# A two-layer trunk on one core: modulation steps moved from the input stage into the attention, and the second layer's weight loads and splits put in another order

## The chip, the cores and the metric

The kernel runs on one core of one Trainium2 chip, as one program of some 28,000 instructions. The metric is device time in microseconds (us), lower is better. The core's engines are PE (TensorE, the matrix products), DVE (VectorE), ACT (ScalarE), POOL (GpSimd) and SP, whose queue issues most of the DMA transfers. Each engine goes through its own list of instructions in order, and waits for the others by semaphores; a transfer queue is gone through in order too.

## The reference

One inference step of two layers over 512 sample tokens and 128 prompt tokens, model width 1024. Layer 0 has latent attention (MLA) with 12 heads, layer 1 a neighbourhood attention with 8 heads beside a windowed attention with 8. Cut to what matters:

```python
def reference(...):
    for l in range(DEPTH):                               # DEPTH = 2
        mp = adaln(c_ctx[None, :], w_mod[l], b_mod[l])   # 6 columns of 1024: mp[:, 0] .. mp[:, 5]
        ms = adaln(c, w_mod[l], b_mod[l])                # (silu(c) @ w_mod + b_mod)
        hp = modulate(rmsnorm(xp, norm_mix[l]), mp[:, 0], mp[:, 1])
        hs = modulate(rmsnorm(xs, norm_mix[l]), ms[:, 0], ms[:, 1])
        op, os_ = ...                                    # in-projection, attention, @ w_out
        xp = xp + mp[:, 2] * op
        xs = xs + ms[:, 2] * os_
        hp = modulate(rmsnorm(xp, norm_ffn[l]), mp[:, 3], mp[:, 4])
        hs = modulate(rmsnorm(xs, norm_ffn[l]), ms[:, 3], ms[:, 4])
        xp = xp + mp[:, 5] * conv_ffn(hp, w_up[l], conv_w[l], conv_b[l], w_down[l])
        xs = xs + ms[:, 5] * conv_ffn(hs, w_up[l], conv_w[l], conv_b[l], w_down[l])
    return rmsnorm(xp, norm_final), rmsnorm(xs, norm_final), ...   # and the new caches
```

## The kernel before

**Layout.** Activations are kept transposed: 128 of the 1024 features in the partitions, 642 columns for the 512 + 128 tokens and two spare ones. They are worked in two halves, 352 and 290 columns in layer 0 (names ending in `a` and `b`, `ha` and `hb`) and 322 and 320 in layer 1. A product of full precision takes a weight and an activation as a high part and a low part: ACT casts the high part (line 117, `whi` from `raw`), and DVE or POOL subtracts it to get the low part (line 113, `wlo`); PE then makes three products (high with high, low with high, high with low).

**The modulation columns.** `w_mod` has 2 layers of 6 columns of 1024, m = 0 to 5. A column cannot be had by an ordinary product without loading PE for one token, so it is summed in *steps*: a step is one load of 128 rows of one column (`mraw`, 512 or 256 wide), and for each of the two conditioning vectors a multiply and an add into `acc`. The first vector's add is one instruction on DVE (line 316). The second vector's is the same on DVE in the form `m.d`, and otherwise a multiply on ACT (line 313) and an add on POOL (line 314). The first step of eight is a multiply only (line 310, ACT). The eighth is followed by a transposition (line 325) and a reduction (line 326) on DVE for each vector, into `mred`. When a column's parts are all reduced, `mod_finish` has PE move them into place (line 337). The list `todo` gives the order of steps. Column m = 2 of layer 0 is needed first in the output product, m = 3 and 4 in the norm after it.

**Layer 0's input stage** (`mla_in`) follows a table of names, `MLA_IN`, written out by hand: one list for all engines, each name issuing a piece of work. `m` and `m.d` issue a modulation step, with loads on ACT's queue; `p` a block of products; `nw.q.0` and `nw.q.1` the norm's factors for the two halves of the query latents; `sc` and `lo` their high and low parts (`qan`); `xc`, `xa`, `xb`, `xm` work on the pooling branch. After the table, `mla` makes the first four query products, whose evacuation on DVE is line 774 (`q` from `tr` and a table) and line 113.

**Layer 0's attention** (`mla`) goes through 26 units (12 heads by two halves, and two more rounds in which the last units drain). Each unit follows one of the two tables `MLA_UNITS`, even or odd. It has one score block (`sc`, maxima at line 808), the exponentials, the turned probabilities (`pt`, line 843) and the weighted sums (`o`, lines 866 and 868). In an even unit `m` stands three times, in an odd one once; from unit 2 on each `m` issues a modulation step, at most `MLA_MODS` = 32 in all, so the units from 18 on issue none. Here the steps are 256 wide and their loads are on SP's queue.

**Layer 0's output product** (`out_proj`) is not written out by hand: a scheduler with its own costs sets the order on the engines. For each of eight `j` it loads `x`, and the weight `wo`, in two rings.

**Layer 1's attention** ends in the table `ODD_END`. `fo` loads an early weight of the output product, `fs` splits it, `pa` splits a group of finished outputs (`o32`) into `ha`, `hb` high and low, in both halves, by `put_act`. After the table the splits that remain are made. **Layer 1's closing stage** is in the class `Mix`: `begin` makes the output product, j = 0 and 1 with the early weights, and j from 2 on with weights loaded by `load` and split by `parts`. Its order of loads is that of the code: x (`load_x`, with a fill of two columns by POOL) and raw weights in turn on SP's queue. The last part of the kernel goes through slots of the up-projection (`slot`), in which `block("S2")` is a block of low parts and `u3` a piece of the convolution on DVE.

## Time and profile before

| what | us |
|---|---|
| runs, median (lowest to highest) | 1706.52 (1704.79 to 1714.16), three runs |
| profiled execution, its own time | 1716.46 |
| its span, first to last instruction | 1714.7, granted clock 0.971 |
| input stage of layer 0, its last part with steps | 93.5 to 142 |
| attention of layer 0, units 2 to 17, with steps | to 308.6 |
| attention of layer 0, units 18 to 25, without | 308.6 to 358 |
| output product of layer 0 | from 358 on |
| layer 1's attention ends, closing stage starts | about 1160 to 1189 |

The profiled execution is about 10 us slower than the median of the runs. A row of a timeline gives the start, the length, the engine, the line, what is written from what, and in brackets how long the engine was idle before it and what ended that idle time. A row of a table by stage gives the stretch, its length, the busy time and the instructions of each engine, the granted clock of PE, the share of the DMA engines and GB/s.

### The profile page before, as it was taken

Reading aid. Unit: us, or ns where it says so; the run is one execution under the profiler, and the core shown is the slowest. Engines: PE = TensorE matmul, PEld = TensorE weight load, DVE = VectorE, ACT = ScalarE, POOL = GpSimd, SP = SyncE. Lnnn points to the kernel's source line nnn. Section 1 sums busy time; section 2 is a strip of 40 time slices with the busy share of each in tenths; the row PEclk is TensorE's granted clock in tenths of the full one; section 3 lists DMA queues with packets and bytes.
Section 4 is the critical chain, followed back from the end, with each engine's and each line's share of the span. In section 5 each row is a group of like instructions: output and inputs, shape, how many; then the busy total and the mean of one; then the engine's idle time right before and its main releaser. Section 6 shows DMA issues by size and latency. Waiting matters only on the chain.

```text
span 1714.7 us, 28130 instructions
## 1 busy us (share of the span) xinstructions
PE 1588.6 (93%) x10349; PEld 1514.9 (88%) x10349; DVE 1266.2 (74%) x2183; ACT 929.1 (54%) x1792; POOL 776.2 (45%) x711
## 2 busy tenths in 40 slices
PE   8877888888999999999998999987997999999996
PEld 2777777788999999999997999986997999999996
DVE  4886788768899778977638777774687667777766
ACT  3554767645655335533445677874465344444435
POOL 2154677554234333433063244655235455555443
PEclk9998999989999999999999999998999999999999
DMA  9431212053344444544235211114222223222221
GB/s 339 136 105 49 62 51 80 13 174 124 117 148 145 153 139 143 155 152 136 68 107 169 59 50 53 50 39 138 86 84 75 78 73 98 82 77 73 78 73 63
DMA packets 79032, 175.62 MB, mean 102 GB/s; under 512 B 11598, under 2 KB 29342, under 8 KB 78894
## 3 DMA queue, kind: packets, MB, share of 16 engines
q1 hardware_dynamic: 76398, 169.55, 30.8%
q10 hardware_dynamic: 2304, 4.20, 0.7%
q8 instruction: 82, 1.34, 0.3%
q14 instruction: 56, 0.46, 0.1%
q0 software_dynamic: 192, 0.07, 0.0%
HBM read 166.71 MB, written 8.03 MB: 102 GB/s over the span
## 4 chain that ended last, share of the span: by engine, by line
PE 54%; DVE 12%; issue 6%; ACT 4%; POOL 3%; DMA 3%; SPq 0%; DVEq 0%; POOLq 0%; ACTq 0%
PE mm L137 26%; PE p L1594 22%; DMA mraw<-in_w_mod_dram 2%; DVE acc L316 1%; PE sc L1209 1%; DVE wlo L113 1%; PE tr L1247 1%; PE o L1259 1%; DVE nt L424 1%; DMA raw<-in_w_out_dram 1%; POOL w L113 1%; DVE ha L438 1%; ACT whi L117 1%; PE sc L137 0%; PE o L851 0%
## 5 line engine op out<-in xcount | busy, mean ns | idle before, releaser
L314 POOL TENSOR_TENSOR acc<-acc,mt 128x512 f32<-128x512 f32 x115 | 175.9, 1530 | 266.3 <-ACT mt L313 251.5
L137 PE MATMUL mm<-ha,whi 128*128 128x352 f32 (+1 forms) x1168 | 288.7, 329 | 4.7 <-ACT ha L437 4.6
L137 PE MATMUL mm<-hb,whi 128*128 128x290 f32 (+1 forms) x1168 | 244.9, 303 | 1.1 <-ACT hb L437 1.1
L137 PEld LDWEIGHTS mm<-ha,whi 128*128 128x128 f32 (+1 forms) x1168 | 203.3, 191 | 6.6 <-ACT ha L437 4.7
L316 DVE SCALAR_TENSOR_TENSOR acc<-mraw,cs,acc 128x512 f32<-128x512 f32 (+1 forms) x165 | 170.5, 1040 | 48.0 <-DMA mraw<-in_w_mod_dram 46.4
L137 PEld LDWEIGHTS mm<-hb,whi 128*128 128x128 f32 (+1 forms) x1168 | 193.6, 192 | 3.9 <-issue 2.7
L137 PE MATMUL mm<-ha,wlo 128*128 128x352 f32 (+1 forms) x584 | 189.5, 325 | 0.0
L113 POOL TENSOR_TENSOR wlo<-raw,whi 128x1024 fp32r<-128x1024 f32 (+3 forms) x47 | 100.5, 2143 | 175.1 <-ACT whi L117 107.2
L137 PE MATMUL mm<-hb,wlo 128*128 128x290 f32 (+1 forms) x584 | 175.2, 300 | 0.0
L113 POOL TENSOR_TENSOR w<-raw,w 128x512 fp32r<-128x512 f32 (+1 forms) x68 | 89.5, 1327 | 177.0 <-ACT w L117 177.0
L137 PE MATMUL mm<-g,whi 128*128 128x352 f32 (+1 forms) x704 | 157.5, 311 | 6.5 <-DVE x L447 5.2
L117 ACT CAST whi<-raw 128x1024 fp32r<-128x1024 f32 (+3 forms) x117 | 115.9, 995 | 69.0 <-PE mm L137 52.7
L313 ACT ACTIVATE mt<-mraw,cs 128x512 f32<-128x512 f32 x115 | 81.8, 721 | 111.7 <-DMA mraw<-in_w_mod_dram 99.4
L1594 PE MATMUL p<-g,d 128*128 128x320 f32 (+1 forms) x912 | 140.4, 312 | 1.0 <-POOL d L113 0.9
L1594 PEld LDWEIGHTS p<-g,d 128*128 128x128 f32 x912 | 136.9, 190 | 2.5 <-POOL d L113 2.1
L1594 PE MATMUL p<-hb,w 128*128 128x322 f32 (+1 forms) x816 | 129.5, 313 | 7.8 <-DVE cg L1965 6.5
L1594 PEld LDWEIGHTS p<-hb,w 128*128 128x128 f32 x816 | 123.5, 191 | 9.0 <-DVE cg L1965 6.8
L1594 PE MATMUL p<-ha,w 128*128 128x322 f32 x768 | 123.0, 315 | 5.8 <-ACT w L117 4.0
L137 PEld LDWEIGHTS mm<-g,whi 128*128 128x128 f32 x704 | 118.3, 189 | 8.6 <-ACT ha L437 3.8
L1594 PEld LDWEIGHTS p<-ha,w 128*128 128x128 f32 x768 | 117.5, 192 | 6.8 <-ACT w L117 4.3
L137 PEld LDWEIGHTS mm<-hb,wlo 128*128 128x128 f32 (+1 forms) x584 | 112.8, 193 | 0.0
L137 PEld LDWEIGHTS mm<-ha,wlo 128*128 128x128 f32 (+1 forms) x584 | 110.4, 189 | 0.5
(332 smaller groups left out, 3773.7 us busy)
## 6 DMA issues: line engine op xcount, KB each, us to landing
raw<-in_w_up_dram SPq DMA_DIRECT2D x90, 512.0 KB, 3.6
mraw<-in_w_mod_dram SPq DMA_DIRECT2D x128, 256.0 KB, 2.9
raw<-in_w_out_dram SPq DMA_DIRECT2D x19, 512.0 KB, 4.2
raw<-in_w_in_odd_dram SPq DMA_DIRECT2D x18, 512.0 KB, 3.5
mraw<-in_w_mod_dram SPq DMA_DIRECT2D x16, 512.0 KB, 8.8
raw<-in_w_down_dram SPq DMA_DIRECT2D x16, 512.0 KB, 3.6
draw<-in_w_down_dram SPq DMA_DIRECT2D x40, 192.0 KB, 2.4
raw<-in_w_down_dram SPq DMA_DIRECT2D x16, 384.0 KB, 3.1
```

Of the source, the lines that this page charges most:

```text
L113: (engine or self.nc.vector).tensor_sub(lo, src, Fv(hi))
L117: self.nc.scalar.copy(hi, src)
L137: self.pe = self.nc.tensor.matmul(out, lhsT=l, rhs=r, start=k == 0, stop=k == n - 1)
L313: nc.scalar.activation(t, raw, AF.Copy, scale=s)
L314: nc.gpsimd.tensor_add(acc, acc, t)
L316: nc.vector.scalar_tensor_tensor(out=acc, in0=raw, scalar=s, in1=acc, op0=ALU.mult, op1=ALU.add)
L424: self.nc.vector.scalar_tensor_tensor(out=t[:, c], in0=x[k][:, c0:c1][:, c], scalar=self.mod[l][:, ma, k, v : v + 1], in1=rs[:, c], op0=AL ...
L438: nc.vector.scalar_tensor_tensor(out=lo[:, c], in0=t[:, c], scalar=ss, in1=Fv(hi[:, c]), op0=ALU.add, op1=ALU.subtract)
L1209: nc.tensor.matmul(ps[:, c : c + n], lhsT=u.Q[:, a], rhs=x[e], start=e == 0, stop=e == 1)
L1247: nc.tensor.transpose(tp[:, j * P : (j + 1) * P], u.p[b][:, x : x + P], self.ident)
L1259: nc.tensor.matmul(u.o[:, u.t[c][2]], lhsT=v, rhs=u.t[c][e], start=c == 0 and e == 0, stop=c == 4 and e == 1)
L1594: self.t.pe = self.nc.tensor.matmul(ps[:, 0:n], lhsT=l_, rhs=r[:, 0:n], start=first and m == 0, stop=last and m == count - 1, skip_group_c ...
```

## The change

- Input stage: the table `MLA_IN` loses eight of its 16 modulation steps (the second half of column 2), on DVE 11 accumulations, two transposes and two reductions. `xc.1` stands earlier and `nw.q.1` behind it, after the first half's low parts.
- Attention of layer 0: `MLA_MODS` goes from 32 to 48. The eight removed steps of 512 columns become 16 of 256, since `todo` gives the second half of column 2 in pieces of 256. They come first there, and all others later in turn, until unit 25. `mod_finish` at unit 2 and after the attention go.
- Output product of layer 0: two x loads at first and each next x ahead, and the raw of a weight loaded one `j` ahead.
- End of layer 1's attention: the second early weight's low part is made on DVE instead of POOL; `pa` splits the first half alone, and the second halves follow after the table, on ACT and DVE.
- Closing stage of layer 1: the three raw weights are loaded before anything else, then the x.
- Slots: the block `S2` comes after `u3`.

```diff
 MLA_IN = """
-f.xp0 ln.c f.wk f.xp1 nw.c.0 m nw.c.1 p.q0.1 ...
+f.xp0 ln.c f.wk f.xp1 nw.c.0 nw.c.1 p.q0.1 ...
...
-MLA_MODS = 32
+MLA_MODS = 48
...
 ODD_END = """
-... t.1 fs.0 pa pl pw pa l.1 po w.0 t.2 fs.1 pa w.1 ...
+... t.1 fs.0 pa pl pw pa l.1 po w.0 t.2 fs.1.d pa w.1 ...
...
     def out_proj(self, pool, l, oT, xsrc, after, early=()):
-        x, w, h, normed = [], [], self.acts(), None
+        x, w, h, normed, raws = [], [], self.acts(), None, list(early)
+
+        def load_x():
+            if len(x) < KT:
+                x.append(self.T(pool, "x", [P, W], F32, 8))
+                nc.sync.dma_start(x[-1], xsrc[:, len(x) - 1, :])
+
+        for _ in range(2):
+            load_x()
...
                     if not half:
-                        xt = self.T(pool, "x", [P, W], F32, 8)
-                        nc.sync.dma_start(xt, xsrc[:, j, :])
-                        x.append(xt)
-                        split = early[j] if j < len(early) else self.fetch(self.i["w_out"][l, j], D, ...)
-                        w.append(split(nc.gpsimd if j in OUT_LO[l] else nc.vector))
+                        load_x()
+                        w.append(raws[j](nc.gpsimd if j in OUT_LO[l] else nc.vector))
+                        if len(raws) < KT:
+                            raws.append(self.fetch(self.i["w_out"][l, len(raws)], D, wpool, ("wo", "wo"), 10))
...
-            if t == 2:
-                self.mod_finish("tr")
...
-                    self.put_act(oT, (put + 4) % 8, o32[put], eng, EVEN)
+                    self.put_act(oT, (put + 4) % 8, o32[put], eng, EVEN, (0,))
...
-                    self.w_first[n] = self.w_first[n](nc.gpsimd)
+                    self.w_first[n] = self.w_first[n](eng)
...
                 for half in range(2):
-                    for n in range(put, 8):
+                    for n in range(0 if half else put, 8):
                         self.put_act(oT, (n + 4) % 8, o32[n], halves=EVEN, only=(half,))
...
-            self.todo = deque(self.mods_of(0, (2,), 512) + self.mods_of(0, (4,), 256) + self.mods_of(0, (3, 5), 512))
+            self.todo = deque(self.mods_of(0, (2,), 512)[:KT] + self.mods_of(0, (2,), 256)[2 * KT :] + ...)
...
                         self.mla(self.ap, oT, wq)
-                        self.mod_finish("tr")
...
+        for j in range(2, 5):
+            load(j, False)
...
-        load_x(0), load_x(1)
-        for j in range(2, 5):
-            load(j)
+        for j in range(5):
+            load_x(j)
...
-        self.u2(f), sums(1), conv("aid"), block("S2")
+        self.u2(f), sums(1), conv("aid")
         self.p7(f)
-        self.u3(f), conv("tapa", "mul"), block("S3")
+        self.u3(f), block("S2"), conv("tapa", "mul"), block("S3")
```

What the change does to the order is seen at three places. First DVE at the end of the input stage, before: the last query latents (`qan`, high and low part on two numbered tiles), two accumulations with the sum for each vector, their transposes and reductions, and then the first evacuations of the query products.

```order
L113 TENSOR_TENSOR qan_450<-z_999,qan_449 128x290
L316 SCALAR_TENSOR_TENSOR acc_182_766<-mraw_1038,cs_95,acc_182_766 128x512
L316 SCALAR_TENSOR_TENSOR acc_183_767<-mraw_1038,cs_95,acc_183_767 128x512
L325 STREAM_TRANSPOSE mt_1194<-acc_182_766 128x512
L326 TENSOR_REDUCE mred_739<-mt_1194 128x16
L325 STREAM_TRANSPOSE mt_1197<-acc_183_767 128x512
L326 TENSOR_REDUCE mred_739<-mt_1197 128x16
L774 TENSOR_TENSOR q_251_1276<-tr_1266,qtab_1215 128x352
L113 TENSOR_TENSOR q_1265<-q_251_1276,q_1264 128x352
```

The same place on DVE after the change (line 774 is line 781 there).

```order
L113 TENSOR_TENSOR qan_450<-z_975,qan_449 128x290
L781 TENSOR_TENSOR q_236_1230<-tr_1220,qtab_1169 128x352
L113 TENSOR_TENSOR q_1219<-q_236_1230,q_1218 128x352
L781 TENSOR_TENSOR q_240_1246<-tr_1236,qtab_1169 128x352
L113 TENSOR_TENSOR q_1235<-q_240_1246,q_1234 128x352
```

The six rows of modulation work between the last latents and the first query are gone.

Second DVE in one of the last units of the attention, before: the turned probabilities (`pt`), the reciprocals of the sums (`s`), the maxima of the scores (`nm`) and the output (`o`).

```order
L866 TENSOR_TENSOR o_850_3778<-o_3741,ot_3780 64x256
L843 TENSOR_TENSOR pt_3789<-tr_3783,pt_3788 128x512
L843 TENSOR_TENSOR pt_3797<-tr_3791,pt_3796 128x512
L823 RECIPROCAL s_3759<-s_3759 128x1 x2
L843 TENSOR_TENSOR pt_3814<-tr_3809,pt_3813 128x384
L808 TENSOR_REDUCE nm_3826<-sc_3828 128x1
```

The same unit on DVE after the change.

```order
L873 TENSOR_TENSOR o_850_3782<-o_3730,ot_3784 64x256
L850 TENSOR_TENSOR pt_3793<-tr_3787,pt_3792 128x512
L850 TENSOR_TENSOR pt_3801<-tr_3795,pt_3800 128x512
L830 RECIPROCAL s_3757<-s_3757 128x1 x2
L316 SCALAR_TENSOR_TENSOR acc_845_3758<-mraw_3656,cs_95,acc_845_3758 128x256
L316 SCALAR_TENSOR_TENSOR acc_845_3758<-mraw_3738,cs_95,acc_845_3758 128x256
L850 TENSOR_TENSOR pt_3818<-tr_3813,pt_3817 128x384
L815 TENSOR_REDUCE nm_3840<-sc_3842 128x1
```

Two accumulations of steps stand ahead of the last turned probabilities of the unit and of the next maxima.

Third SP's queue at the start of layer 1's closing stage, before, with the semaphores that each transfer waits for: a store of the new cache, then x and raw weights.

```order
L1024 DMA out_na_v_dram<-kvo_12901 128x128 [waits DMAHW5_49,Activation_49]
L1672 DMA x_13241<-x_mid 128x642 [waits PE_49,Pool_49]
L1672 DMA x_13244<-x_mid 128x642
L1677 DMA raw_13247<-in_w_out_dram 128x1024 [waits DMAHW0_49]
L1672 DMA x_13249<-x_mid 128x642 [waits DMAHW1_49]
L1677 DMA raw_13252<-in_w_out_dram 128x1024 [waits DMAHW2_49]
```

The same queue after the change.

```order
L1029 DMA out_na_v_dram<-kvo_12945 128x128 [waits DMAHW5_49,Activation_49]
L1681 DMA raw_13266<-in_w_out_dram 128x1024 [waits DMAHW4_49,DVE_49]
L1681 DMA raw_13268<-in_w_out_dram 128x1024 [waits DMAHW0_49,Pool_49]
L1681 DMA raw_13270<-in_w_out_dram 128x1024 [waits DMAHW3_49,Pool_49]
L1676 DMA x_13291<-x_mid 128x642 [waits DMAHW1_49,PE_49]
L1676 DMA x_13294<-x_mid 128x642 [waits DMAHW2_49,PE_49]
```

The raws now stand ahead of x, and wait for DVE and POOL instead of for PE.

More of the change, by code (lines that the diff above doesn't have):

```diff
@@ L49 @@
 m p.kr.0 m.d p.c0.0 p.kr.1 r.q0 f.q2 m.d rt p.c0.1 zc.c0 m.d m.d cx p.c1.0 p.c1.1 p.q0.0 sq.c0 zc.c1 r.q1 m.d sq.c1 sm.c r.q2 m.d m.d
-f.xp0 ln.c f.wk f.xp1 nw.c.0 m nw.c.1 p.q0.1 p.q1.0 zc.q0 sq.q0 sc.c.1.0 p.q1.1 sc.c.1.1 lo.c.1.1 sc.c.0.1 r.wk p.q2.0 sc.c.0.0 rc
-lo.c.0.0 zc.q1 lo.c.0.1 sq.q1 lo.c.1.0 m.d r.xp0 kp.1 kp.0 ke.1 p.q2.1 f.wq m.d r.xp1 f.wv ke.0 xz m zc.q2 p.xp0.0 m sq.q2 m sm.q p.xp0.1
-ln.q r.wv nw.q.0 xc.0 xa.0 sc.q.0.0 p.xp1.0 r.wq p.xp1.1 iv.0 sc.q.0.1 xb.0 lo.q.0.0 sc.q.0.2 lo.q.0.1 nw.q.1 lo.q.0.2 m.d xm.0 sc.q.1.0
-sc.q.1.1 xc.1 lo.q.1.0 sc.q.1.2 lo.q.1.1 xa.1 lo.q.1.2 xb.1 iv.1 m.d xm.1
+f.xp0 ln.c f.wk f.xp1 nw.c.0 nw.c.1 p.q0.1 p.q1.0 zc.q0 sq.q0 sc.c.1.0 p.q1.1 sc.c.1.1 lo.c.1.1 sc.c.0.1 r.wk p.q2.0 sc.c.0.0 rc
+lo.c.0.0 zc.q1 lo.c.0.1 sq.q1 lo.c.1.0 r.xp0 kp.1 kp.0 ke.1 p.q2.1 f.wq r.xp1 f.wv ke.0 xz zc.q2 p.xp0.0 sq.q2 sm.q p.xp0.1
+ln.q r.wv nw.q.0 xc.0 xa.0 sc.q.0.0 p.xp1.0 r.wq p.xp1.1 iv.0 sc.q.0.1 xb.0 lo.q.0.0 sc.q.0.2 lo.q.0.1 xc.1 lo.q.0.2 nw.q.1 xm.0 sc.q.1.0
+sc.q.1.1 lo.q.1.0 sc.q.1.2 lo.q.1.1 xa.1 lo.q.1.2 xb.1 iv.1 xm.1
 """
@@ L84 @@
 ODD_END = """
-fo.0 fo.1 t.0 pt l.0 pa t.1 fs.0 pa pl pw pa l.1 po w.0 t.2 fs.1 pa w.1 t.3 l.2 t.4 pa l.3 je w.2 w.3 pa l.4 w.4 o
+fo.0 fo.1 t.0 pt l.0 pa t.1 fs.0 pa pl pw pa l.1 po w.0 t.2 fs.1.d pa w.1 t.3 l.2 t.4 pa l.3 je w.2 w.3 pa l.4 w.4 o
 """
@@ L458, in out_proj @@
                     if not half:
-                        xt = self.T(pool, "x", [P, W], F32, 8)
-                        nc.sync.dma_start(xt, xsrc[:, j, :])
-                        x.append(xt)
-                        split = early[j] if j < len(early) else self.fetch(self.i["w_out"][l, j], D, *(() if j < 3 else (wpool, ("wo", "wo"), 10)))
-                        w.append(split(nc.gpsimd if j in OUT_LO[l] else nc.vector))
+                        load_x()
+                        w.append(raws[j](nc.gpsimd if j in OUT_LO[l] else nc.vector))
+                        if len(raws) < KT:
+                            raws.append(self.fetch(self.i["w_out"][l, len(raws)], D, wpool, ("wo", "wo"), 10))
                     ps = self.PS("mm")
@@ L1496, in run @@
             nc.vector.tensor_scalar(out=self.nsink, in0=self.sink, scalar1=-1.0, scalar2=None, op0=ALU.mult)
-            self.todo = deque(self.mods_of(0, (2,), 512) + self.mods_of(0, (4,), 256) + self.mods_of(0, (3, 5), 512))
+            self.todo = deque(self.mods_of(0, (2,), 512)[:KT] + self.mods_of(0, (2,), 256)[2 * KT :] + self.mods_of(0, (4,), 256) + self.mods_of(0, (3, 5), 512))
             oT = self.acts()
```

## The prediction

> **What bounds the kernel now.** I read the page first (busy shares), then a table by stage over the places that the change touches, then the timelines of the engines at those places.
>
> ```profile
> span 1714.7 us, 28130 instructions
> PE 1588.6 (93%) x10349; PEld 1514.9 (88%) x10349; DVE 1266.2 (74%) x2183; ACT 929.1 (54%) x1792; POOL 776.2 (45%) x711
> ```
>
> PE is busy for 93% of the span, so 126 us is all that can be won without taking products away, and this change takes none away. The next table says where PE is idle; its columns are length, busy time of each engine (count), granted clock, DMA share, GB/s.
>
> ```profile
> core 0: us, PE busy (x) PEld busy (x) DVE busy (x) ACT busy (x) POOL busy (x), PEclk, DMA share, GB/s
> 93.50:142.00 48.50, 34.22 (x188) 32.05 (x189) 43.18 (x50) 19.71 (x38) 32.92 (x30) 0.82 0.41 126
> 142.00:308.60 166.60, 142.22 (x959) 129.28 (x957) 127.72 (x269) 116.45 (x275) 113.03 (x114) 0.97 0.16 51
> 308.60:326.50 17.90, 13.95 (x86) 12.48 (x87) 13.12 (x29) 9.55 (x22) 6.91 (x9) 0.90 0.01 2
> 326.50:338.00 11.50, 9.68 (x70) 8.71 (x69) 8.73 (x20) 7.92 (x20) 5.24 (x5) 1.00 0.13 46
> 338.00:358.00 20.00, 17.78 (x113) 15.96 (x112) 11.57 (x25) 10.74 (x26) 10.26 (x16) 0.91 0.16 46
> 1160.00:1189.00 29.00, 19.10 (x79) 15.97 (x79) 9.77 (x17) 12.58 (x29) 15.25 (x20) 0.76 0.27 89
> 1189.00:1330.00 141.00, 128.37 (x819) 125.52 (x820) 99.17 (x169) 81.63 (x165) 52.87 (x41) 0.96 0.30 101
> 1330.00:1660.00 330.00, 329.82 (x2217) 328.61 (x2216) 236.34 (x400) 145.45 (x257) 176.91 (x136) 1.00 0.25 79
> ```
>
> Two stretches run badly: the end of layer 0's input stage (93.5 to 142: DVE 43 of 48.5 us busy, PE 34 at a clock of 0.82) and the start of layer 1's closing stage (1160 to 1189: PE 19 of 29 at 0.76). Both are edited. From 1330 on PE idles 0.18 of 330 us: nothing can be won there, and nothing given back by an engine that still keeps up.
>
> **A: eight modulation steps leave the input stage.** The end of the stage as PE sees it: the rows that begin after an idle time, with the idle time and its releaser in brackets.
>
> ```profile
> 105.78 0.83 PE L359 MATMUL b<-sqz,ones 128*128 128x352 f32 x2 [2.79 <-DVE sqz L404]
> 122.87 0.43 PE L137 MATMUL tr<-qan,whi 128*128 128x352 f32 x1 [1.92 <-DVE qan L113]
> 128.27 0.95 PE L137 MATMUL tr<-qan,whi 128*128 128x352 f32 x2 [4.81 <-ACT px L683]
> 136.45 0.85 PE L137 MATMUL tr<-qan,whi 128*128 128x290 f32 x2 [3.95 <-DVE q L774]
> ```
>
> And as DVE goes through the last of it, then the steps' share of DVE in the whole stretch (accumulations L316, the two transposes L325, the two reductions L326):
>
> ```profile
> 122.05 0.77 DVE L113 TENSOR_TENSOR qan<-z,qan 128x352 fp32r<-128x352 f32 x1
> 122.74 3.49 DVE L316 SCALAR_TENSOR_TENSOR acc<-mraw,cs,acc 128x512 f32<-128x512 f32 x2
> 129.82 3.46 DVE L316 SCALAR_TENSOR_TENSOR acc<-mraw,cs,acc 128x512 f32<-128x512 f32 x2
> 135.88 0.51 DVE L774 TENSOR_TENSOR q<-tr,qtab 128x352 f32<-128x352 f32 x1
> 93.50:136.00 42.50, 15.10 (x11) 0.86 0.35 108
> 93.50:136.00 42.50, 1.40 (x2) 0.86 0.35 108
> 93.50:136.00 42.50, 1.37 (x2) 0.86 0.35 108
> ```
>
> The four waits sum to 13.5 us (2.79 + 1.92 + 4.81 + 3.95). All but the third are put down to DVE. The third is put down to ACT, whose work was long done; what ran just before on DVE is the 3.49 us of steps at 122.74, ahead of the half-1 `z` and `qan`. The last follows from what DVE does between 129.82 and 135.88: six instructions of steps stand in a row ahead of the first `q` evacuation, and PE can go on only when one of those products has left its bank.
>
> What goes: 15.10 + 1.40 + 1.37 = 17.9 us of DVE work. How much of it is on the path? The second-half norm chain (`nw.q.1`) moves behind the first half, and `xc.1` ahead of it: a rearrangement among instructions that all remain, costed at 0. The first `q` evacuation at 135.88 can come earlier by at most the 17.9 us. DVE then still needs, for the same stretch, 42.5 − 17.9 = 24.6 us, of which a few are waits for PE's sums (105.78 waits for DVE, and DVE for PE in turn). I take 13: the size of the four waits, which is what PE has to give; about 4 us of the DVE work removed was in DVE's own slack. The ends are −17 (nearly all of DVE's 17.9) and −9 (the two last waits, 8.8, alone). Part of the gain is in PE's clock: after the wait a pair of `qan` products takes 0.85, and in a run without waits 0.43.
>
> ```profile
> 131.52 0.43 PE L137 MATMUL tr<-qan,whi 128*128 128x290 f32 x2
> ```
>
> The Trainium skill has a rule for this ("TensorE: Matmul & The Clock Gate", section "What's actually happening"): PE falls to half its clock after an idle window of about 3.4 us. The trace agrees as far as 0.85 against 0.43; by that rule alone each avoided wait would be worth up to 1.7 us more than its length, which for the two long ones would make the sum 3 us better, an estimate.
>
> Also removed here: two first steps on ACT, three multiplies on ACT, three adds on POOL, and eight loads on ACT's queue. None of these engines ends a wait above except by way of DVE: 0.
>
> **B: sixteen steps come into the first attention.** The steps there now come three in each even unit and one in each odd unit, and stopped at the 18th of 26 units; they will go on to the last. They are 256 wide. Added: 14 accumulations on DVE, 16 activations and 2 first steps on ACT, 14 adds on POOL, 4 transposes and 4 reductions on DVE, and 16 more loads on SP's queue. Rows of the same steps in the earlier units (count, then min/median/max ns), two pairs of units that carry eight steps, and DVE after the last unit:
>
> ```profile
> L316 DVE SCALAR_TENSOR_TENSOR acc<-mraw,cs,acc x28: 454/1114/1619, 168.4 to 304.0; 128x256 f32<-128x256 f32 x28
> L314 POOL TENSOR_TENSOR acc<-acc,mraw x28: 718/734/1001, 173.6 to 306.1; 128x256 f32<-128x256 f32 x28
> L325 DVE STREAM_TRANSPOSE mraw<-acc x8: 444/446/447, 200.6 to 307.8; 128x256 f32<-128x256 f32 x8
> 237.00:256.00 19.00, 15.15 (x95) 13.68 (x96) 15.40 (x33) 13.45 (x31) 11.60 (x13) 0.91 0.13 42
> 256.00:273.00 17.00, 14.83 (x110) 13.65 (x109) 14.44 (x31) 12.21 (x30) 13.20 (x15) 1.00 0.20 63
> 359.87 2.53 DVE L113 TENSOR_TENSOR wo<-raw,wo 128x1024 fp32r<-128x1024 f32 x1 [4.25 <-issue]
> ```
>
> In the units without steps, 308.6 to 358, DVE is busy 13.12 + 8.73 + 11.57 = 33.4 of 49.4 us. The steps add between 14 × 0.454 + 8 × 0.446 = 9.9 and 14 × 1.114 + 3.6 = 19.2 us (a reduction taken as a transpose). In two pairs that carry steps DVE reaches 15.40/19 = 81% and 14.44/17 = 85% of the time. At 85% the stretch would take (33.4 + 9.9)/0.85 = 50.9 to (33.4 + 19.2)/0.85 = 61.9 us, so +1.5 to +12.5; at the middle 56.4, +7. The last accumulation and the four closing instructions, 1 + 4 × 0.446 = 2.8 us, fall into DVE's idle 4.25 us ahead of `wo`, leaving about +4. I take +4, with 0 and +9 as ends (below 0 is excluded: nothing is taken out of these units). ACT and POOL have room: 28.2 and 22.4 us busy of 49.4, and 9 and 10.3 more. SP's 16 loads put `w_uv`, `w_qk` and one `w_out` load behind loads that wait for a free step buffer; DMA share there is 0.01 to 0.16 and each weight is used units later: 0.
>
> The column finished in the input stage had its two PE moves at unit 2; they now come at a later unit, and the closing ones of column 4 come inside the output product instead of before it: 8 tiny products each, 0.
>
> **C: the output product of layer 0.** Two x loads at first and one raw weight fetched ahead. The rows after an idle time:
>
> ```profile
> 381.90 10.01 PE L137 MATMUL mm<-ha,wo 128*128 128x352 f32 x46 [3.64 <-DVE wo L113]
> 403.09 1.89 PE L337 MATMUL b<-mred,sel 128*128 128x16 f32 x8 [4.74 <-DVE mred L326]
> ```
>
> The 3.64 us is the seventh weight, whose load stands in SP's queue behind loads of modulation raws; the order moves it past one x load only, with the same raws ahead. The 4.74 us is the last reduction of the next column, unchanged. I take −0.5; ends −3 (most of the first wait) and +3 (the same wait again, at another weight).
>
> **D and E: the end of layer 1's attention and the start of its closing stage.** The rows of PE, ACT, SP's queue, POOL and DVE around it:
>
> ```profile
> 1170.09 0.74 PE L1594 MATMUL p<-ha,whi 128*128 128x322 f32 x2
> 1176.97 0.64 PE L1594 MATMUL p<-ha,whi 128*128 128x322 f32 x1 [0.95 <-POOL ha L113]
> 1188.42 0.57 PE L1594 MATMUL p<-ha,w 128*128 128x322 f32 x2 [3.99 <-ACT w L117]
> 1187.23 1.14 ACT L117 CAST w<-raw 128x512 fp32r<-128x512 f32 x2 [14.33 <-DMA raw<-in_w_out_dram]
> 1181.02 0.42 SPq L1677 DMA_DIRECT2D raw<-in_w_out_dram x1
> 1179.61 0.26 POOL L1673 MEMSET x<- 128x2 f32 x6 [1.98 <-PE p L1594]
> 1166.38 1.05 ACT L117 CAST whi<-raw 128x1024 fp32r<-128x1024 f32 x1
> 1176.88 0.74 POOL L113 TENSOR_TENSOR hb<-o,hb 128x320 fp32r<-128x320 f32 x1
> ```
>
> Layer 1's first two products are made from weights loaded early, 1170.09 to 1184.43. The third weight is loaded at 1181.02: its issue stands on SP behind two x loads, and these wait until PE has read the early weights, whose place x takes (POOL's fill of x waits for PE at 1179.61 for the same reason). The raw lands 6.2 us later (1187.23), is split in 1.2 us, and PE starts at 1188.42.
>
> After: the raws are issued first, into the places of the attention's own raws, which come free when the second early weight has been split. That split's low part is now DVE's instead of POOL's: DVE can begin it when ACT's cast ends (1166.38 + 1.05) and needs at most 2.53 (a split of 1024 columns, in the row at 359.87), so it ends near 1169. A raw issued at 1169 and landing 6.2 us later is there at 1175; its split waits for DVE's splits of the activation halves and stands at about 1178. POOL is rid of that split and of the second halves' low parts (six of 0.74 or more), so the early products no longer wait for it, and their end comes some 5 us earlier, at 1179. The third product can then start at 1179 instead of 1188.4: −9. Ends: −12 (the early products end at 1176) and −4 (the raw takes 11 us because x's loads and three raws share the DMA rings, or the splits queue on ACT and DVE). What is put off, the second halves' splits, is eight splits of some 0.74 on each of ACT and DVE, due only when the products of half 1 start, after all those of half 0: 0. The low part now on DVE stands ahead of the last score's low parts: a loss of up to 1, in the −9. That it is kept to the end is seen in PE's 128.37 of 141 and 329.82 of 330: PE has little room behind it to lose the gain in.
>
> **F: the place of one block of DVE work.**
>
> ```profile
> 1324.83 3.59 PE L1594 MATMUL p<-hb,w 128*128 128x322 f32 x12 [6.49 <-DVE cg L1965]
> ```
>
> In the first slot PE waits 6.49 us for a chain on DVE; `S2` now stands behind `u3` and still ahead of what ends that wait. In the other slots PE is fully busy. −0.5; ends −3 and +2.
>
> **Sum.** −13 + 4 − 0.5 − 9 − 0.5 = −19. The profiled execution took 1716.5 us (span 1714.7 and 1.8 around it), giving 1697.5; it lies 10 us above the median of the three runs, 1706.5, which I carry along: 1687.5.
>
> **The rivals.** R1, slower: in the attention's last units DVE and POOL cannot overlap, and the 16 steps serialise. Their work is 19.2 + 10.3 = 29.5 us; less the 2.8 covered that is +27 in place of +4, and 1710.5. It decides once a step costs above 23/16 = 1.44 us net. For it speaks that an accumulation of 256 columns takes 454 ns at the least and 1114 at the median. Against it: 237 to 256 holds 15.40 of DVE and 11.60 of POOL, 27 us, in 19. The page "SBUF — State Buffer" of the Trainium skill ("Who interferes with whom") states that a DVE instruction with two inputs in SBUF and a GpSimd instruction that reads SBUF lock each other out; the spread of 454 to 1114 agrees with it, and the overlapped pair limits it.
>
> R2: the input stage keeps its length. DVE's steps were filling time in which PE, POOL and ACT made the next inputs; only the last wait of 3.95 goes, so −4 in place of −13: 1696.5. For it: the third wait names ACT, and POOL has 33 of 48.5 us.
>
> R3: the closing stage gives its gain back: the raws land no sooner, since the split that frees their place is queued on DVE, or x arrives late for the first sums. 0 in place of −9: 1696.5. For it: raw and x share the queue and took 6.2 us.
>
> R4: R2 and R3 together, or an unseen shift of places in SBUF: 1705.5, no change.
>
> **How the numbers follow.** The likeliest has 0.58; R2 0.17, R3 0.14, R4 0.08, R1 0.03. Within 0.5% (8.5 us, about what a measurement of this kernel tells from no change) lie R4 and small parts of R2 and R3, 0.11; slower by more is R1's upper part and what I have not seen, 0.03; faster 0.86. The likeliest's own terms run to −13 − 4 + 4 − 4 − 9 − 3 − 1 = −30 at the one side, of which I keep −28, 1678; R2 and R3 reach to 1697, with their own errors 1700. The range is 1678 to 1700.
>
> **What would show it.** A: no DVE steps after the first column, the first `q` evacuation near 122, the attention's first scores near 129. B: unit pairs of 17 to 19 us to the end, and the sum of the last four pairs about 4 us longer. C: the waits of 3.64 and 4.74 still there in some form. D, E: the third output product of layer 1 starts about 9 us sooner, counted from the first early product (1170.09), and ACT's 14.33 us wait for the raw is short. F: the 6.49 stays within 1. The forecast fails most simply if the first scores come less than 9 us sooner, or the last four units lose over 9.

## The result, and the profile after

Over 18 runs each the kernel before took 1711.4 us (1704.8 to 1715.8) and the changed one 1701.6 us (1698.2 to 1704.8); the ratio is 0.9940, with a 95% interval of 0.9932 to 0.9948. The change gains 10 us where 19 were forecast, and 1701.6 lies just above the range. (The three runs shown at first had a median 5 us below that of the 18, so 5 us of the miss in the absolute time is the base; the 9 us in the gain are not.) The profiled executions, 1716.5 and 1702.5, lie 14 apart, 4 more than the medians: single profiles differ by a few us, so each place below is told with several kernels' profiles.

The page of the changed kernel, and PE at the two places of the prediction, as rows of the timeline. Column by column: start, length, engine, line, what is done, and in brackets the idle time before and its releaser.

```profile
span 1700.7 us, 28202 instructions
PE 1582.5 (93%) x10349; PEld 1510.7 (89%) x10349; DVE 1263.7 (74%) x2197; ACT 934.2 (55%) x1805; POOL 780.0 (46%) x715
...
123.92 0.61 PE L137 MATMUL tr<-qan,whi 128*128 128x290 f32 x1 [4.79 <-ACT qan L636]
126.64 0.61 PE L137 MATMUL tr<-qan,whi 128*128 128x290 f32 x1 [2.11 <-DVE qan L113]
...
377.96 8.97 PE L137 MATMUL mm<-ha,wo 128*128 128x352 f32 x46 [3.14 <-DVE wo L113]
400.51 1.86 PE L337 MATMUL b<-mred,sel 128*128 128x16 f32 x8 [6.85 <-DVE mred L326]
427.18 0.76 PE L359 MATMUL b<-sq,ones 128*128 128x290 f32 x2 [0.34 <-DVE sq L404]
...
1168.66 0.74 PE L1598 MATMUL p<-ha,whi 128*128 128x322 f32 x2
1176.17 16.04 PE L1598 MATMUL p<-ha,w 128*128 128x322 f32 x106
1311.22 3.59 PE L1598 MATMUL p<-hb,w 128*128 128x322 f32 x12 [6.69 <-DVE cg L1970]
```

The closing stage of layer 1 does what was forecast. The early products start at 1168.66 and the late ones at 1176.17, without a wait, 7.5 us apart; before they were 18.3 apart (1170.09 and 1188.42). The input stage gains too: of its four waits of 13.5 us there are left two of 6.9 together, and two short ones of 0.39 and 0.78. But at 427 the two kernels stand at the same time (to a hundredth, which is chance, since single profiles differ by a few us): the row of 427.18 has its counterpart before in this one.

```profile
427.17 0.76 PE L359 MATMUL b<-sq,ones 128*128 128x290 f32 x2 [0.85 <-DVE sq L404]
```

In this pair everything that layer 0 won is gone by the end of its output product. The next table follows it. Each row is one stretch: from the first query evacuation (end of the input stage) to the output product's first matmul, and from there to the row above at 427. The first pair is the kernel before, the second the changed one.

```profile
135.88:354.30 218.42, 185.48 (x1225) 168.28 (x1226) 164.48 (x346) 145.30 (x344) 135.73 (x139) 0.95 0.15 48
354.30:427.17 72.87, 63.65 (x396) 62.13 (x396) 57.06 (x86) 38.11 (x60) 39.62 (x43) 0.91 0.53 175
```

```profile
127.90:349.35 221.45, 185.22 (x1223) 167.82 (x1222) 174.88 (x361) 153.44 (x362) 148.92 (x152) 0.95 0.19 59
349.35:427.18 77.83, 66.32 (x406) 64.34 (x406) 61.52 (x93) 38.31 (x61) 41.12 (x45) 0.91 0.47 157
```

The input stage ends 8.0 sooner (135.88 to 127.90). The attention takes 3.0 longer and the output product 5.0 longer. DVE is busy for 10.4 us more in the attention and 4.5 more in the product: 14.9 us, of which 8.0 show as length.

### The profile page after: what moved, and what is told of

It reads as the page before. It is cut to its first block, busy times and chain, and to the rows that moved or that the text cites. A ratio compares the mean times of both kernels' runs of the same rounds, so it can differ in the third digit from the quotient of the medians.

```text
span 1700.7 us, 28202 instructions
## 1 busy us (share of the span) xinstructions
PE 1582.5 (93%) x10349; PEld 1510.7 (89%) x10349; DVE 1263.7 (74%) x2197; ACT 934.2 (55%) x1805; POOL 780.0 (46%) x715
## 4 chain that ended last, share of the span: by engine, by line
PE 55%; DVE 13%; issue 5%; ACT 4%; DMA 2%; POOL 1%; SPq 0%; DVEq 0%; ACTq 0%; POOLq 0%
PE mm L137 26%; PE p L1598 24%; DMA mraw<-in_w_mod_dram 2%; DVE acc L316 2%; PE sc L1214 1%; DVE wlo L113 1%; PE o L1264 1%; PE tr L1252 1%; DVE nt L424 1%; DVE ha L438 1%; ACT whi L117 1%; DVE v L2001 1%; DVE w L113 0%; DVE x L447 0%; DVE pt L113 0%
```

## The experiments

All runs were timed against the kernel before on the same chip. Four asked which part of the change carries the 10 us.

**The parts of the change alone.** `e1_close` has only D and E:

```diff
-... t.2 fs.1 pa w.1 ...
+... t.2 fs.1.d pa w.1 ...
...
-                    self.put_act(oT, (put + 4) % 8, o32[put], eng, EVEN)
+                    self.put_act(oT, (put + 4) % 8, o32[put], eng, EVEN, (0,))
...
+        for j in range(2, 5):
+            load(j, False)
...
-        load_x(0), load_x(1)
-        for j in range(2, 5):
-            load(j)
+        for j in range(5):
+            load_x(j)
```

> The kernel before with only the layer-1 parts (fs.1.d, second halves split last, raws ahead of x in Mix.begin). Theory T1 (the gain of the change is made at the start of layer 1's closing stage; what the input stage wins is given back by the end of layer 0's output product): 1701 to 1703 us against 1711, ratio 0.9940 to 0.9950, the third output product of layer 1 about 18.5 us after the last early start of before is reached 10 to 12 us sooner. Rival T2 (both ends win about half, so that closing stage alone gives 4 to 6): ratio 0.9965 to 0.9977.

Measured: 1702.3 us, ratio 0.9939 (0.9921 to 0.9957). That is the whole of the change's gain.

`e2_steps` has only A and B:

```diff
-f.xp0 ln.c f.wk f.xp1 nw.c.0 m nw.c.1 p.q0.1 ...
+f.xp0 ln.c f.wk f.xp1 nw.c.0 nw.c.1 p.q0.1 ...
...
-MLA_MODS = 32
+MLA_MODS = 48
...
-            self.todo = deque(self.mods_of(0, (2,), 512) + ...
+            self.todo = deque(self.mods_of(0, (2,), 512)[:KT] + self.mods_of(0, (2,), 256)[2 * KT :] + ...
...
```

> The kernel before with only the modulation steps moved (MLA_IN, MLA_MODS = 48, todo, the two mod_finish). T1: the first scores 8 us sooner, the output product's start about 5 us sooner, the first product of the first up-projection at the same time within 1.5 us; time 1709 to 1713, ratio 0.999 to 1.001. T2: the 5 us stay to the end: 1706, ratio 0.997.

Measured: 1713.7, ratio 1.0008 (0.9997 to 1.0019).

`e3_wout` has only C:

```diff
+        for _ in range(2):
+            load_x()
...
+                            raws.append(self.fetch(self.i["w_out"][l, len(raws)], D, wpool, ("wo", "wo"), 10))
...
```

> The kernel before with only the new order of loads in layer 0's output product. T1: same within 1.5 us, ratio 0.999 to 1.001. Rival T3 (the new order of loads itself costs what the input stage wins, since it moves raw loads of column 3 on SP's queue): 3 to 5 us slower, ratio 1.002 to 1.003.

Measured: 1714.8, ratio 1.0016 (1.0004 to 1.0029): a loss of some 1 to 5 us, on its own, between the ranges of T1 and T3.

`e4_layer0` has A, B and C:

```diff
-MLA_MODS = 32
+MLA_MODS = 48
...
+        for _ in range(2):
+            load_x()
...
```

> The kernel before with the steps moved and the new order of loads in the output product, without the layer-1 parts. T1: ratio 0.999 to 1.001. T2: 0.997 or better. T3: above e2 by 0.002 to 0.003.

Measured: 1712.0, ratio 0.9995 (0.9984 to 1.0007). So T1 holds on the main point: layer 0's three parts bring nothing together, layer 1's two parts bring all. The stretches of `e2_steps`, which has the old output product, show that the product is longer without C too:

```profile
127.45:348.11 220.66, 182.20 (x1223) 164.85 (x1222) 176.49 (x361) 153.75 (x362) 148.35 (x152) 0.96 0.19 59
348.11:424.39 76.28, 65.01 (x406) 62.72 (x407) 62.30 (x93) 38.56 (x61) 39.78 (x45) 0.93 0.49 160
```

**Where layer 0 gives it back.** Two kernels leave out half of column 3 (8 of its 16 steps; the second half of its sums is a copy of the first), one of the kernel before and one of the changed kernel:

```diff
...
-self.mods_of(0, (3, 5), 512))
+self.mods_of(0, (3,), 512)[:KT] + self.mods_of(0, (5,), 512))
```

> The kernel before with half of column m = 3 left out (8 of its 16 steps, the second half of its sums is a copy of the first). T1 in its sharper form (T1a: in the output product the 16 steps of column 3 end at a time that does not follow the product's start, PE waits for them, and this eats what is won ahead of it): PE's wait at the column's move falls from 4.7 to under 1 us, time 1707 to 1710, ratio 0.997 to 0.9985. Rival T1b (the column is no gate, what is won is lost by DVE in the half after it): ratio 0.999 to 1.0005, the second half takes up the wait.

Measured: 1711.1 us, ratio 0.9988 (0.9977 to 0.9998), a little less gain than T1a's range.

> The changed kernel with the same half of column 3 left out. T1a: the input stage's gain now passes the output product: 4 to 6 us below the changed kernel beyond what the same cut brings the kernel before, that is a ratio of 0.989 to 0.991. T1b: the same distance to the cut kernel before as the changed kernel has to the kernel before (0.006), so 0.993 to 0.9945.

Measured: 1696.5, ratio 0.9909 (0.9893 to 0.9925). The cut alone brings the kernel before some 2 us and the changed kernel about 5, so the distance between the two grows from 10 to 13.5 us (0.9909 / 0.9988 = 0.992). That growth of 3.5 us is about as large as its own uncertainty. In both PE's wait at the column's move is gone, and the product is no longer lengthened by the change, as the two stretches show (before with the cut, then changed with the cut):

```profile
352.52:422.49 69.97, 61.30 (x397) 59.86 (x396) 56.83 (x86) 36.09 (x58) 37.41 (x41) 0.95 0.53 174
```

```profile
349.46:417.51 68.05, 62.74 (x404) 61.69 (x404) 57.59 (x91) 36.09 (x57) 34.03 (x41) 0.94 0.52 172
```

So the column in the output product probably takes part of the gain, some 3.5 us of it, as T1a says, whose range the ratio just meets. The cut also takes eight steps off DVE, so it does not tell the wait for the column from DVE's work on it.

Three kernels tried to take the wait away without leaving work out.

```diff
-self.mods_in(pool, len(self.todo), 2, nc.sync)
+self.mods_in(pool, len(self.todo), 3, nc.sync)
```

> The changed kernel with three places instead of two for the raws of modulation steps from the output product on. T1a with loads as the pace of the column: the wait at the column's move falls from 6.9 to 2 to 4 us, ratio 0.991 to 0.9925. If the steps' place in the engines' order is the pace: 0.9935 to 0.9945 as the changed kernel.

Measured: 0.9958 (0.9943 to 0.9974), outside both ranges: no gain and perhaps a loss of 3. PE's wait at the column's move did fall, from 6.85 to 0.47, but waits for DVE's evacuations came in its place:

```profile
396.32 1.04 PE L337 MATMUL b<-mred,sel 128*128 128x16 f32 x8 [0.47 <-DVE mred L326]
416.27 3.45 PE L137 MATMUL mm<-hb,wo 128*128 128x290 f32 x24 [3.09 <-DVE x L447]
348.44:425.13 76.69, 63.99 (x404) 61.45 (x404) 69.06 (x97) 40.20 (x64) 48.35 (x48) 0.95 0.54 176
```

DVE is busy for 69.1 of 76.7 us here, 90%, with 97 instructions against 93 in the changed kernel. The loads were not the only pace; with more of them in flight DVE is close to the bound of the stage.

```diff
-MODS_OUT = 2
+MODS_OUT = 3
```

> The changed kernel with three modulation steps per product group in the output product instead of two. T1a with the order as the pace: the column ends earlier, ratio 0.991 to 0.9925. With loads as the pace: the steps wait on DVE and hold up the evacuations, ratio 0.994 to 0.996.

Measured: 0.9949 (0.9935 to 0.9964), inside the range for the loads as the pace, and the wait is still 6.7: a third step in each group does not bring the column sooner when only two loads are in flight.

```diff
-OUT_LO = [(1, 3, 5, 7), range(8)]
+OUT_LO = [range(8), range(8)]
```

> The changed kernel with all low parts of layer 0's output weights on POOL instead of four on POOL and four on DVE. If DVE's work bounds the output product after the change (its busy share there is about 80%): 2 to 4 us below the changed kernel, ratio 0.9915 to 0.993. If the longer split on POOL (2.4 us) gates PE instead, or takes the port from DVE: the same or slower, 0.994 to 0.996.

Measured: 0.9969 (0.9957 to 0.9981), 5 us worse than the changed kernel, and worse than both ranges. PE now waits for a split on POOL, and the column's move starts 4.5 later (404.99 against 400.51):

```profile
378.31 3.79 PE L137 MATMUL mm<-ha,wo 128*128 128x352 f32 x22 [1.39 <-POOL wo L113]
404.99 1.86 PE L337 MATMUL b<-mred,sel 128*128 128x16 f32 x8 [7.35 <-DVE mred L326]
```

Yet in this profile the output product as a whole is as long as in the changed kernel's (77.61 against 77.83 us). So the second expectation, that the splits on POOL gate PE, is not shown by it, and where the 5 us are lost stays open.

**What the steps cost, by leaving them out.** The new input stage, and the eight steps nowhere (the second half of column 2 is a copy of the first); attention and output product as before:

```diff
...
-self.mods_of(0, (2,), 512) + self.mods_of(0, (4,), 256)
+self.mods_of(0, (2,), 512)[:KT] + self.mods_of(0, (4,), 256)
```

> The kernel before with the new input stage and without the eight steps anywhere (the second half of column 2's sums is a copy of the first); attention and output product as before. Upper bound of the input stage's gain: first query evacuation near 128, output product's start 7 to 8 us sooner. T1a (the column with its 16 steps and DVE at the output product eat part): 1706 to 1709, ratio 0.9965 to 0.998. T2 (all survives): 0.9955 or less. If the product eats all: 0.9995.

Measured: 1706.3, ratio 0.9965 (0.9951 to 0.9978), which is −6.0 us (−3.8 to −8.4). Its stretches have the lengths of before:

```profile
128.65:345.34 216.69, 183.94 (x1230) 166.75 (x1230) 164.75 (x346) 145.41 (x345) 136.93 (x139) 0.96 0.15 47
345.34:418.55 73.21, 64.43 (x396) 62.88 (x396) 55.21 (x86) 37.89 (x60) 38.78 (x43) 0.90 0.53 174
```

This decides against the idea that the output product swallows any gain made ahead of it: an earlier start passes it almost whole. What eats the 6 to 8 us are the steps where they now stand. Over the profiles of five kernels with the steps in the attention's last units (the changed one, `e2`, `e4`, `e7`, `e8`) attention and product together take 296.9 to 299.3 us, and over five without them (before, `e1`, `e3`, `e9`, `e10`) 287.4 to 291.3: 8 us more, about half in each.

Three last runs asked whether it matters where the steps end. First the moved steps kept 512 wide, so that the attention has 40 and ends them at unit 21:

```diff
-MLA_MODS = 48
+MLA_MODS = 40
...
-self.mods_of(0, (2,), 512)[:KT] + self.mods_of(0, (2,), 256)[2 * KT :] + ...
+self.mods_of(0, (2,), 512) + ...
```

> The changed kernel with the eight moved steps kept 512 wide, so that 40 steps instead of 48 stand in the attention and end at unit 21. T4 (what the attention's steps cost is its own 4 us and another 4 us because steps end with the last unit and load DVE, ACT and POOL at the start of the output product): the spill of 4 goes and the attention is no longer, 3 to 5 us below the changed kernel, ratio 0.991 to 0.9925. Rival T5 (the cost goes by bytes summed on DVE and POOL, not by where they end): ratio 0.9935 to 0.9945.

Measured: 0.9938 (0.9926 to 0.9951). T4 is refuted as a way to gain, and the ratio lies in the range of its rival T5. The place of the cost does follow the steps: in one profile each the product is shorter by 3.4 than in the changed kernel and the attention longer by 1.2, its units 3 to 17 by 3.6 (134.4 against 130.8) with the last ones shorter.

```profile
127.64:350.31 222.67, 184.65 (x1230) 167.31 (x1230) 173.59 (x357) 150.95 (x354) 149.50 (x146) 0.96 0.17 55
350.31:424.79 74.48, 64.28 (x396) 62.42 (x395) 58.68 (x86) 37.70 (x60) 39.27 (x43) 0.91 0.53 171
```

Then column 4's moves back at the end of the attention:

```diff
                         self.mla(self.ap, oT, wq)
+                        self.mod_finish("tr")
```

> The changed kernel with the moves of column 4 (mod_finish) back at the end of the attention instead of inside the output product. If those eight small products and the half clock around them are the first 1.5 us of the spill: about 1 us less, ratio 0.993 to 0.9937, the first product of the late weights 12 us behind the product's start instead of 13.4. If they only move: 0.994, with a wait of PE at the end of the attention.

Measured: 1701.2, ratio 0.9934 (0.9920 to 0.9948). The product is 6.7 shorter than in the changed kernel and the attention 5.7 longer: the work moves and the sum stays. The ratio lies in the range for 1 us less, which the intervals do not tell from none.

```profile
127.23:354.33 227.10, 183.21 (x1231) 165.86 (x1230) 176.91 (x370) 157.56 (x369) 153.22 (x160) 0.96 0.20 62
354.33:425.44 71.11, 64.53 (x396) 63.15 (x396) 59.89 (x88) 36.08 (x58) 39.75 (x40) 0.92 0.52 169
```

And the steps added without the change of the input stage, with half of column 3 as their work:

```diff
-MLA_MODS = 32
+MLA_MODS = 48
...
-self.mods_of(0, (3, 5), 512))
+self.mods_of(0, (3,), 256)[: 2 * KT] + self.mods_of(0, (3,), 512)[KT:] + self.mods_of(0, (5,), 512))
```

> The kernel before with its input stage as it was and 16 more steps of 256 columns in the attention all the same: half of column 3, which the output product then does not need to sum. It prices the 16 steps alone. T4: the attention 4 to 5 us longer, the output product 2 us shorter for its eight steps less and longer for steps that end with the last unit: ratio 1.001 to 1.003. If the steps are hidden: 0.998 to 0.999, as with half of column 3 left out.

Measured: 1719.5, ratio 1.0034 (1.0023 to 1.0046). Sixteen steps in these units cost 6 us in time, though the output product has eight steps less to do and is 3.2 shorter in this profile (69.7 against 72.9); a little worse than T4's range.

**Which half of the closing stage.** Only the splits' order at the end of layer 1's attention:

```diff
...
-                    self.put_act(oT, (put + 4) % 8, o32[put], eng, EVEN)
+                    self.put_act(oT, (put + 4) % 8, o32[put], eng, EVEN, (0,))
...
-                    self.w_first[n] = self.w_first[n](nc.gpsimd)
+                    self.w_first[n] = self.w_first[n](eng)
...
```

> The kernel before with only the end of layer 1's attention changed (second halves split last, the second early weight's low part on DVE), x and raws in the old order. If the load order is what matters (my forecast's step E): the early products end some 3 to 5 us sooner, but the third still waits for a raw issued behind x: 0 to 4 us, ratio 0.998 to 1.000. If the early end of the early products frees x's place and so the raws (rival): 5 us or more, ratio below 0.997.

Measured: 0.9986 (0.9974 to 0.9998). And only the raws first:

```diff
+        for j in range(2, 5):
+            load(j, False)
...
-        load_x(0), load_x(1)
-        for j in range(2, 5):
-            load(j)
+        for j in range(5):
+            load_x(j)
```

> The kernel before with only the raw weights ahead of x at the start of layer 1's closing stage. If the load is the whole gate: 4 us, the length of PE's wait for the third weight (3.99), ratio 0.9975; the early products keep their waits for POOL and their half clock. If both parts are needed: less than 3 us, ratio above 0.998. If this alone does it: 0.994 to 0.995.

Measured: 0.9972 (0.9961 to 0.9983). The parts bring 2.4 and 4.8 us alone, together 10.4 (`e1_close`, whose interval is 7.4 to 13.5). The plain sum of 7.2 lies just below that, so some of the gain seems to need both, which the intervals do not settle. The profiles point the same way: from the first early product to the first late one it is 18.3 us before, 13.9 with the splits alone (1166.72 to 1180.58), 13.7 with the raws alone (1167.22 to 1180.96) and 7.5 in the changed kernel. The rows of each say what each leaves undone. With the splits alone (first row, then SP's issue of the first raw) PE is through its early products and waits 5.2 us for a raw issued behind x. With the raws alone (last row) PE does not wait for a raw, and it is held by POOL's splits:

```profile
1180.58 14.67 PE L1594 MATMUL p<-ha,w 128*128 128x322 f32 x77 [5.20 <-ACT w L117]
1173.53 0.42 SPq L1677 DMA_DIRECT2D raw<-in_w_out_dram x1
```

```profile
1172.31 0.64 PE L1594 MATMUL p<-ha,whi 128*128 128x322 f32 x1 [1.32 <-POOL ha L113]
```

## Why the prediction was wrong, step by step

**D and E: −9, right.** Alone they bring 10.4 (7.4 to 13.5), and the late products start 10.8 sooner counted from the first early one. The raws are issued at 1165.96 in the changed kernel, ahead of x, and the early products run without a wait:

```profile
1165.96 1.28 SPq L1681 DMA_DIRECT2D raw<-in_w_out_dram x3
1173.54 2.18 ACT L117 CAST w<-raw 128x512 fp32r<-128x512 f32 x4
```

The raw is split at 1173.5 and used at 1176.2; I had 1178 and 1179. The gain passes to the end as argued, and R3 is out.

**A: −13, mis-sized; measured −8 in the stage and −6 in time where the steps are dropped.** The step that failed is "13: the size of the four waits". The first query evacuation comes at 127.90 where 122 was forecast, and the first scores start 8.1 us sooner (134.01 against 142.12), less than the 9 that the forecast had set itself. The first wait (2.79) is gone and the second (1.92) is down to 0.39 and 0.78, but the two long ones are still there with another cause, as 4.79 and 2.11. In the place of the removed steps DVE now does the second half's norm chain beside POOL's work, and three of its rows take longer:

```profile
118.19 2.28 DVE L380 TENSOR_SCALAR r<-r 128x290 f32<-128x290 f32 x1
120.51 1.43 DVE L381 TENSOR_TENSOR r<-r,r 128x290 f32<-128x290 f32 x1
121.97 2.88 DVE L634 SCALAR_TENSOR_TENSOR z<-z,gq,r 128x290 f32<-128x290 f32 x2
117.94 2.37 POOL L113 TENSOR_TENSOR wlo<-raw,whi 128x1024 fp32r<-128x1024 f32 x1
120.26 1.36 POOL L696 TENSOR_TENSOR ps<-px 128x663 f32<-128x663 f32 x1
```

The same rows before, and POOL beside the first two of them:

```profile
120.71 0.79 DVE L380 TENSOR_SCALAR r<-r 128x290 f32<-128x290 f32 x1
121.53 0.59 DVE L381 TENSOR_TENSOR r<-r,r 128x290 f32<-128x290 f32 x1
126.16 0.94 DVE L627 SCALAR_TENSOR_TENSOR z<-z,gq,r 128x290 f32<-128x290 f32 x2
119.94 1.39 POOL L707 TENSOR_TENSOR o<-o,px 128x512 f32<-128x512 f32 x1
121.29 0.52 POOL L706 TENSOR_TENSOR o<-ps,inv 128x128 f32<-128x128 f32 x1
128.29 1.29 POOL L689 TENSOR_TENSOR ps<-px 128x663 f32<-128x663 f32 x1 [3.27 <-ACT px L683]
```

The three rows took 0.79, 0.59 and 0.94 before and take 2.28, 1.43 and 2.88 now, 4.3 us more, during which POOL goes through its split and its shifted sums without an idle time. Before, the `z` pair had stood at 126.16, in an idle time of POOL (the 3.27 of the last row). POOL was not idle beside the first two rows, but its rows there were shorter. In both kernels each of the two ends 0.2 to 0.3 us after the POOL row beside it (120.47 after 120.31 now, 121.50 after 121.33 before), so in these rows the cost goes by the length of the POOL row that is met.

The rule of the Trainium skill that the prediction named beside R1 ("SBUF — State Buffer", "Who interferes with whom") bears on it: by that page a `tensor_scalar` can enter a mode that takes the port shared with GpSimd, and a DVE instruction with two inputs in SBUF contends with a GpSimd instruction that reads SBUF. The rows agree with it. I had costed the moved `nw.q.1` at 0; that is the second thing wrong in A. The lower end of my range, −9, came of the two last waits and was still too large by 1.

A third is my reading of the 4.81 us wait. ACT's work was not long done there: its copy of `px`, which stood in ACT's order behind the second half's first casts, ended at 128.22, and PE went on at 128.27. After the change it is done by 116.29.

```profile
127.95 0.27 ACT L683 COPY px<-mm 128x128 f32<-128x128 f32 x1
116.02 0.27 ACT L690 COPY px<-mm 128x128 f32<-128x128 f32 x1
```

So the move of `xc.1`, which I had costed at 0, had a part in freeing PE there, and not the leaving of the steps alone. How large a part is open, since no run has that move by itself.

**B: +4, met in the attention by luck, and too small by 4 in all.** Over the same ten profiles the attention is 3.8 us longer with the steps (220.7 to 222.7 against 216.0 to 218.4), inside 0 to +9, but two errors cancel in it. The next rows are the attention's first units (0 to 2) and its last (from 18 on, until the output product starts), before and then changed.

```profile
142.12:174.30 32.18, 26.81 (x157) 24.09 (x156) 16.89 (x38) 18.21 (x46) 14.42 (x15) 0.89 0.02 5
303.90:354.30 50.40, 42.21 (x275) 37.67 (x274) 35.91 (x76) 29.69 (x71) 24.21 (x27) 0.93 0.03 11
```

```profile
134.01:162.30 28.29, 22.71 (x149) 20.01 (x148) 16.85 (x37) 18.16 (x46) 14.46 (x15) 1.00 0.06 20
293.10:349.35 56.25, 44.07 (x268) 39.32 (x266) 46.24 (x91) 37.56 (x88) 35.95 (x40) 0.89 0.17 53
```

The last units, where the steps went, are 5.9 us longer in this pair and 6.6 over the ten profiles. That is close to the +7 that I had before taking 2.8 off, so the step that failed is that "the last accumulation and the four closing instructions" are covered because they "fall into DVE's idle 4.25 us". They do fall there (350.80 to 354.63), but the units ahead of them are longer all the same, and that idle time was also the lead of the output product. The first units are 3.9 us shorter in this pair and 2.6 over the ten. There the eight small products that move column 2 had stood, at unit 2; they now come at 240.29, and I had costed their going at 0. With the new input stage, but these products still at unit 2, `e11_dropped` takes 30.5 us for the first units, against 28.2 to 29.7 in all profiles without them there. The score products behind them ran at 0.73 us a pair, and at 0.45 after the change:

```profile
158.20 1.48 PE L337 MATMUL tr<-mred,sel 128*128 128x16 f32 x8
160.20 0.73 PE L137 MATMUL sc<-kh,q 128*128 128x320 f32 x2
150.82 0.45 PE L137 MATMUL sc<-kh,q 128*128 128x320 f32 x2
```

The other 4 us are in the output product, which I had at 0. The late moves stand inside it (`e14_finish` moves them out, and the attention grows instead), the first late weight comes 13.5 instead of 11.7 us after the product's start, and column 3's end comes 51 instead of 49 us after it. PE's wait for that column is no measure of it: it is 6.85 in the changed kernel and 4.74 before, but 4.16 in `e2_steps`, whose product is long too.

**C: −0.5, inside its ends of −3 and +3, but not the sign.** Alone it costs 0.16%, some 3 us; beside A and B no cost could be measured. Both of its waits are still there. **F: −0.5.** The wait is 6.69 against 6.49; it was not run alone.

So the rival nearest to the truth was R2's number (1696.5 on the old base; −10) but not its mechanism: I had the input stage gain 4 and the attention lose 4, and measured is 8 gained and 8 given back. R1's mechanism, DVE and POOL that do not overlap, is partly what happened: 14.9 us of DVE's added work made 8.0 of length, and R1's deciding price of 1.44 us a step was not reached (8/16 = 0.5). Adding 16 steps without any gain ahead is a loss (`e15_steps_added`, +6 us).

What stays open is why the attention and product together lose 8 us, and not the 4 of the attention alone, wherever the steps and their moves end (`e13_512`, `e14_finish`). That DVE's work sets it, in stages where it is busy for 75 to 79% of the time, fits all rows, but no run took work from DVE in the attention alone. ACT and POOL are busier by 7.9 and 11.7 us in the last units too, and PE's granted clock is 0.89 there where it was 0.93, so DVE is not the only candidate.

No version run here beats the changed kernel by more than its interval: `e14_finish` has 0.9934 and `e13_512` 0.9938 against its 0.9940, and the layer-1 parts alone (0.9939) are as good.

## What to carry to other kernels

Work that was moved out of one tight stage into another cost there what it saved. So compare the busy share of the engine that does the work in both stages, and price the work where it lands with what runs beside it, the stage behind it included. A chain that moves into the place of removed work meets a different neighbour on the other engine, so its instructions' old lengths do not carry over. When a forecast of a stage comes out right, look at its parts: here +6.6 and −2.6 stood behind a +4. Order of loads was different: raws issued before the fill that waits for PE, and splits put off that nobody needs yet, showed no cost and gave all of the 10 us.

## What was not expected of the hardware

How much a neighbour on POOL costs a short instruction of DVE. The same `TENSOR_SCALAR` of 128 x 290 took 2.28 us in the input stage, and 0.31 in the norm behind the output product of the same kernel, where POOL had been idle for 6.84 us until 432.41:

```profile
431.44 0.31 DVE L380 TENSOR_SCALAR r<-r 128x290 f32<-128x290 f32 x1
432.41 1.52 POOL L314 TENSOR_TENSOR acc<-acc,mt 128x512 f32<-128x512 f32 x1 [6.84 <-ACT mt L313]
```

The loads' pace is also a matter of how many are in flight: with three places instead of two PE's wait for the column fell from 6.85 to 0.47 us, and DVE's share of the output product rose to 90%, with no gain.
